# A decoder layer on one core: gate tiles as paired block products ahead of the attention, keys a head sooner, batched small operations

## The chip, the cores and the metric

The kernel runs on one core of a Trainium2 chip. The metric is the device time of one execution in microseconds; the median of three runs is compared. The engines are TensorE (PE, matmuls into PSUM), VectorE (DVE), ScalarE (ACT), GpSimd (POOL) and SyncE (SP, which issues most of the DMAs).

## The reference

One layer of a hybrid decoder over 1024 tokens with 1024 channels, in float32, with three branches that read one input projection, are gated and merged:

```python
h = rms_norm(x, norm_mix_pre[l])
proj = h @ w_in[l]
q_d, k_d, v_d, u_p, q_m, gate_logits = jnp.split(proj, split_pts, axis=-1)
...
a = diff_attention(q_d, k_d, v_d, lam)               # 8 heads, two softmax maps each, ALiBi, causal
a = rms_norm(a, subln_g[l]) * (1.0 - lam_init)
y_attn = a.reshape(B, S, DIFF_V_WIDTH).astype(x.dtype) @ w_attn_branch[l]
...
gates = jax.nn.sigmoid(gate_logits.astype(jnp.float32)).reshape(B, S, N_BRANCHES, D).astype(x.dtype)
mix = gates[:, :, 0] * y_attn + gates[:, :, 1] * y_pool + gates[:, :, 2] * y_mem
x = x + rms_norm(mix @ w_out[l], norm_mix_post[l])
```

`diff_attention` forms, per head and block of queries, two softmax maps p0 and p1 over the keys and weighs the values with p0 - lam * p1. A second half, the channel mixer (up projection, depthwise convolution of width 3, gelu gate, down projection), follows; the change doesn't touch it.

## The kernel before

**Number format.** Every large matmul is done in three passes: each operand is split into a high part (ScalarE copy to the fp32r format, line 89) and a low part (VectorE subtraction, line 90), and `mm3` (lines 102 to 105) adds high x high, high x low and low x high into PSUM. A split costs one instruction on each of the two engines.

**Stages, in order.** (1) Norm of `x` and `mem`, keys and values of the memory branch; (2) memory attention and the pooling projection; (3) the pooled and the memory branch; (4) the gates of those two branches (lines 861 to 881); (5) values of the attention (lines 957 to 997), and under them the key weights of heads 2 to 7, split and stored to DRAM (`key_weights`, line 922); (6) keys of heads 0 and 1, queries of all heads, gate tiles 0 and 1 of the attention branch (lines 1019 to 1033); (7) the attention, head by head (lines 1273 to 1346); (8) the rest of the gates, the norm of the heads and the merge (lines 1366 to 1420); (9) output projection and channel mixer.

**Block products.** Stages 4 to 6 use `seven` (line 198): a pair of 128-channel tiles times all tokens as a 2 x 2 block product with seven products instead of eight, with sums of the weights and of the tokens. Each product takes a page of 512 weights per partition, splits it, and issues 4 blocks of `mm3`. `channels` (line 999) loads the two weight tiles of a pair (`rawq`; one slot in `wst`'s tag `raw`, which has two, one in `grp`) and calls `seven`. A tile done directly (`gate`, line 1116, and `head_keys`, line 1090) takes for each half of the tokens 8 blocks of `mm3`.

**Attention.** Each head has four query blocks of 256 queries, each of two tiles of 128. `scores` (line 1140) does for one tile and both maps the matmuls into `pss`, a VectorE operation that adds the bias and takes the extreme (line 1165), and the exponential on ScalarE with its sum (line 1170). `combine` (line 1176) joins the maps of one tile with two operations on one column (lines 1181, 1182) and one over all keys (1184). `turn_weights` transposes and splits the weights (`pta`, `aT`), `weigh_values` multiplies them with `v` (`poa`), `head_norm` sums squares over channels (`pn`). `weave` spreads "fillers" between these stages: the keys of the next head (four steps of 12 matmuls), the loads of its values, and gate steps of 6 matmuls. `GATES` (line 1290) puts gate tiles 2 and 3 into head 0 and tile 4 into head 7.

**Behind the attention.** Gate tiles 5 to 7 run directly (line 1370). Each head's output `a` and its norm factor `rb`, both from DRAM, are multiplied (line 1384) and split into `ath` and `atl`. The factors of heads 4 to 7 go through `load_norms` (`hn`), about 15 small VectorE operations in `head_norms`, and a store to `r_d`, before `rb` can be read. `merge_heads` (line 1356) multiplies with `w_attn_branch`, one 128-channel tile `dt` at a time, first half of the heads (g = 0) and then the second; only tiles 0 and 1 have their first half issued ahead of the second four heads. `merge` (line 1403) gates the result, adds the other branches and splits.

**What sets the order.** The kernel is written in one order; a planner then places each instruction on its engine's queue as early as its inputs and buffers allow, with program order as the priority, so PE's gate matmuls slip into places where the attention's are not ready. `issue_after` puts an instruction behind a named one on the same engine: gate matmuls stay behind the scores that were written before them. DMAs issued by SP wait in SP's queue, one behind the other.

**Memory.** Pools are stacked; the attention's pools `qkp` (32 KB a partition: four key tiles, two query tiles), `att` and `vp` (two buffers of values of 8 KB) are closed behind it, and `atp` (`ath`, `atl`, 64 KB), then `sub` (`a` and `rb`, four buffers of 4 KB each) take their place from the same upper end down; a tile waits for the tiles on whose bytes it lies.

Of the kernel before, what the change touches and what calls it, by code (L numbers as in the profile page):

```python
# [41 lines left out]
def kernel(  # L42
# [275 lines left out]
    wk_d = dram.tile([NH, P, 2, KT, P], F32, name="wk_d")  # L318
    v_d = dram.tile([NH, P, 2, KT, P], F32, name="v_d")
# [541 lines left out]
    with tc.tile_pool(name="gp", reuse_waits="tile", bufs=2, side="right") as gp_:  # L861
# [60 lines left out]
        def key_weights(h):  # L922

            raw = wst.tile([P, KT, P], F32, tag="raw", name="rawk", bufs=2)
            with tc.issue_after(loads["v"].ins):
                nc.sync.dma_start(out=raw, in_=chunk(w_in, C_K + h * P))
            for e in range(2):
                page = wst.tile([P, 2, H4, P], F32R, tag=("wh", "wl")[pages[0] % 2], name="kpage")
                pages[0] += 1
                ks = slice(e * H4, (e + 1) * H4)  # L930
                split(page[:, 0], page[:, 1], raw[:, ks])
                nc.sync.dma_start(out=wk_d[h, :, :, ks], in_=page.bitcast(F32))
# [92 lines left out]

        ss = gp_.tile([P, 4, H4, P], F32, tag="g", name="ss", bufs=3)
# [4 lines left out]
        ready = {2: wsplit(chunk(w_in, C_G + 2 * P), [P, KT, P])}  # L1031
        with tc.issue_after(ready[2][2].ins):
            late[0]()
# [10 lines left out]
    bias = ap_.tile([P, 1152], F32, name="bias", bufs=1)  # L1044
# [5 lines left out]
    def head_bias(h):  # L1050
        biases[h] = ap_.tile([P, 1152], F32, tag="hbias", name="hbias", bufs=2)
        nc.scalar.activation(out=biases[h], in_=bias, func=AF.Copy, scale=2.0 ** -(h + 1))
# [26 lines left out]
    def key_tiles(h):  # L1079
        return [qkp.tile([P, S], F32R, tag="ks%d%d" % (c, h % 2), name="ks%d" % c) for c in range(2)]  # L1080
# [9 lines left out]
    def head_keys(h):  # L1090
# [25 lines left out]
    def gate(dt):  # L1116


        with tc.issue_after(last["load"].ins):
            wh, wl, _ = ready.pop(dt) if dt in ready else wsplit(chunk(w_in, C_G + dt * P), [P, KT, P])  # L1120
        for i in range(2):
# [18 lines left out]
    def scores(h, b, u):  # L1140
# [9 lines left out]
        sm = small.tile([P, 1], F32, tag="sm", name="sm")  # L1150
# [5 lines left out]
        for c in range(2):  # L1156
            pss = bank2(name="pss2")
            for i in range(parts):
                keys = ks[c][:, i * m:(i + 1) * m]
                for j in range(2):  # L1160
                    last["scores"] = nc.tensor.matmul(pss[:, i * H:i * H + m], q[:, j, c, ts], keys,  # L1161
                                                      start=(j == 0), stop=(j == 1))
            z = ap_.tile([P, S], F32, tag="z%d" % c, name="z", bufs=3 - c)
# [7 lines left out]
                                 bias=mx[:, c:c + 1], accum_out=sm if c else sums[:, h, t:t + 1])  # L1171
        exps[h, b, u] = z2, mx, sm
# [3 lines left out]
    def combine(h, b, u):  # L1176

        z2, mx, sm = exps.pop((h, b, u))
        t = 2 * b + u
        n = (t + 1) * P  # L1180
        nc.vector.reciprocal(out=mx[:, 1:2], in_=sm)
        nc.vector.scalar_tensor_tensor(
            out=mx[:, 0:1], in0=mx[:, 1:2], scalar=sums[:, h, t:t + 1], in1=nlam, op0=ALU.mult, op1=ALU.mult)
        last["combine"] = nc.vector.scalar_tensor_tensor(
            out=z2[0][:, 0:n], in0=z2[1][:, 0:n], scalar=mx[:, 0:1], in1=z2[0][:, 0:n],
            op0=ALU.mult, op1=ALU.add)
        zts[h, b, u] = z2[0]
# [89 lines left out]
    first = gate(2)  # L1277
# [8 lines left out]
    with tc.issue_after(last["load"].ins):  # L1286
        ready[3] = wsplit(chunk(w_in, C_G + 3 * P), [P, KT, P])
        for dt in range(2):
            nc.sync.dma_start(out=gate_d[dt], in_=g01[dt])
    GATES = ((2, 3), (), (), (), (), (), (), (4,))  # L1290
    blocks = [(h, b) for h in range(NH) for b in range(4)]
    for h in range(NH):
        stages = []
        for b in range(4):
# [10 lines left out]
            if n >= 1:  # L1305
                def weights(n=n):
                    combine(*blocks[n - 1], 1)
# [3 lines left out]
            stages.append(lambda h=h, b=b: combine(h, b, 0))  # L1311
# [15 lines left out]
        fillers = []  # L1327
        if h + 1 < NH:
            if h:
                fillers += steps(head_keys(h + 1), 4)  # L1330
            for n, step in enumerate(steps(values(h + 1), 2)):
                fillers.insert(2 * n + 1, step)
        n = 0
        for dt in GATES[h]:
            for step in steps(first if dt == 2 else gate(dt), 6 if dt == 2 else 8):
                fillers.insert(min(n, len(fillers)), step)
                n += 2
        weave(stages, fillers)
    combine(*blocks[-1], 1)
# [5 lines left out]
    load_norms(1)  # L1345
# [8 lines left out]
    pys = {}  # L1354

    def merge_heads(dt, g):
# [441 lines left out]
```

## Time and profile before

| what | value |
|---|---|
| median of three runs (lowest, highest) | 1727.77 us (1726.58, 1728.74) |
| span of the profiled execution | 1727.6 us |
| PE busy | 1712.8 us (99%) |
| VectorE busy | 1241.3 us (72%) |
| ScalarE busy | 886.6 us (51%) |
| attention, first scores to last values | 605.3 to 881.8 us |
| first merge matmul | 910.8 us |

The profiled execution's own time is the span, first to last instruction; the runs' times are measured without the profiler's page and lie around it by less than 1.2 us. In the rows of the timeline the columns are start, duration, engine, line, operation, output<-inputs, shapes and count, with idle time and its releaser in brackets. In rows that begin with a:b, a stretch of the span, the columns are its length, the busy time and number of instructions of PE, PE's weight loads, VectorE, ScalarE and GpSimd, then the granted clock, the share of the DMA engines' time and GB/s. Rows that begin with a line number are groups: durations are the least, the median and the most in ns, then the first and the last start. A matmul's recorded duration overlaps with the next one's.

### The profile page before, as it was taken

To read this page: it belongs to the slowest core of one execution; us is meant where nothing else is said; L and a number is where in the kernel's file an instruction comes from. 1 tells how busy PE (TensorE), PEld (TensorE's weight loads), DVE (VectorE), ACT (ScalarE), POOL (GpSimd) and SP (SyncE) were. 2 spreads that over 40 slices of the span, in tenths; PEclk is the share of its full clock that TensorE was granted. 3 is DMA by queue.
4 is the path that set the end of the run, shared out by engine and by line. 5 is a ranking of instruction groups with operands and counts; after the bars stand their busy time and mean duration, and the time that the engine had idled before them with its cause. 6 is when DMAs were issued, how large, how long until landed. Compare 5 with 4: busy or idle time off the path is not lost.

```text
span 1727.6 us, 22400 instructions
## 1 busy us (share of the span) xinstructions
PE 1712.8 (99%) x8106; PEld 1421.4 (82%) x8106; DVE 1241.3 (72%) x2047; ACT 886.6 (51%) x1577; POOL 45.0 (3%) x103
## 2 busy tenths in 40 slices
PE   9999999999999999999999999999999999999998
PEld 7888888887888888888888888888888888888886
DVE  6765875666665578888866555848888888878466
ACT  5434544434544467777754344645555555543453
POOL 0000000000000011111110000000000000000000
PEclk9999999999999999999999999999999999999999
DMA  8873544444874686665556571572333423583344
GB/s 273 317 281 114 163 150 133 166 147 143 266 237 159 201 231 170 176 182 152 145 187 239 176 230 50 171 225 92 124 112 107 122 85 98 190 299 106 107 149 142
DMA packets 232803, 294.41 MB, mean 170 GB/s; under 512 B 15865, under 2 KB 161526, under 8 KB 230006
## 3 DMA queue, kind: packets, MB, share of 16 engines
q1 hardware_dynamic: 229158, 285.61, 51.8%
q0 software_dynamic: 3520, 7.38, 1.2%
q8 instruction: 64, 1.05, 0.3%
q14 instruction: 45, 0.37, 0.1%
q10 hardware_dynamic: 16, 0.00, 0.0%
HBM read 201.10 MB, written 85.56 MB: 166 GB/s over the span
## 4 chain that ended last, share of the span: by engine, by line
PE 91%; DVE 5%; DMA 2%; ACT 1%; issue 1%; SPq 0%; DVEq 0%; ACTq 0%
PE pa L103 8%; PE pa L104 8%; PE pa L105 8%; PE pb L103 5%; PE pb L104 5%; PE pb L105 5%; PE pss L1161 3%; PE poa L1217 2%; PE pd L103 2%; PE pd L105 2%; PE pd L104 2%; PE pe L105 2%; PE pe L104 2%; PE pe L103 2%; PE pout L103 2%; PE pout L105 2%
## 5 line engine op out<-in xcount | busy, mean ns | idle before, releaser
L89 ACT ACTIVATE wpage<-s 128x512 fp32r<-128x512 f32 x136 | 85.3, 627 | 108.2 <-DVE s L188 35.3
L90 DVE TENSOR_TENSOR wpage<-s,wpage 128x512 fp32r<-128x512 f32 x136 | 92.8, 688 | 43.2 <-ACT wpage L89 43.2
L1565 DVE SCALAR_TENSOR_TENSOR cvt<-gv,cols,cvt 128x1023 f32<-128x1023 f32 x88 | 112.5, 1278 | 15.6 <-ACT cvt L1561 14.9
L1165 DVE CUSTOM_DVE_ANT_0 z<-pss,hbias 128x256 f32<-128x256 f32 (+7 forms) x128 | 94.5, 752 | 26.0 <-PE pss L1161 24.8
L1170 ACT ACTIVATE z<-z,mx 128x256 f32<-128x256 f32 (+7 forms) x128 | 98.8, 773 | 20.8 <-DVE mx L1165 20.7
L103 PE MATMUL pa<-T,wpage 128*128 128x512 f32 x264 | 102.8, 389 | 0.0
L105 PE MATMUL pa<-T,wpage 128*128 128x512 f32 x264 | 102.7, 389 | 0.0
L104 PE MATMUL pa<-T,wpage 128*128 128x512 f32 x264 | 102.7, 389 | 0.0
L1161 PE MATMUL pss<-ks,q 128*128 128x512 f32 (+5 forms) x384 | 86.6, 349 | 1.4 <-DVE mx L1165 1.4
L89 ACT ACTIVATE page<-blk 128x1024 fp32r<-128x1024 f32 (+1 forms) x42 | 41.4, 989 | 85.7 <-PE pe L104 50.6
L90 DVE TENSOR_TENSOR page<-blk,page 128x1024 fp32r<-128x1024 f32 (+1 forms) x42 | 47.5, 1130 | 38.1 <-ACT page L89 38.1
L1161 PEld LDWEIGHTS pss<-ks,q 128*128 128x128 f32 x384 | 62.9, 189 | 11.1 <-DVE mx L1165 6.2
L103 PE MATMUL pd<-page 128*128 128x512 f32 x176 | 68.7, 390 | 0.0
L104 PE MATMUL pd<-page 128*128 128x512 f32 x176 | 68.5, 389 | 0.0
L105 PE MATMUL pd<-page 128*128 128x512 f32 x176 | 68.3, 389 | 0.0
L103 PE MATMUL pa<-hT,wpage 128*128 128x512 f32 x168 | 65.5, 390 | 0.1
L105 PE MATMUL pa<-hT,wpage 128*128 128x512 f32 x168 | 65.4, 389 | 0.0
L104 PE MATMUL pa<-hT,wpage 128*128 128x512 f32 x168 | 65.4, 389 | 0.0
L1217 PEld LDWEIGHTS poa<-aT,v 128*128 128x128 f32 x480 | 60.7, 190 | 3.0 <-ACT srow L1237 1.4
L1217 PE MATMUL poa<-aT,v 128*128 128x256 f32 (+1 forms) x480 | 62.5, 280 | 0.0
L103 PEld LDWEIGHTS pa<-T,wpage 128*128 128x128 f32 x264 | 49.6, 188 | 10.7 <-DVE gv L250 0.3
L104 PEld LDWEIGHTS pa<-T,wpage 128*128 128x128 f32 x264 | 49.6, 188 | 10.2
(429 smaller groups left out, 4965.7 us busy)
## 6 DMA issues: line engine op xcount, KB each, us to landing
q<-q_d SPq DMA_DIRECT2D x64, 256.0 KB, 5.1
wd<-in_w_down_dram SPq DMA_DIRECT2D x22, 512.0 KB, 5.0
tw_d<-wd SPq DMA_DIRECT2D x11, 1024.0 KB
rawv<-in_w_up_dram SPq DMA_DIRECT2D x22, 512.0 KB, 5.8
rawu<-in_w_up_dram SPq DMA_DIRECT2D x22, 512.0 KB, 4.1
ff_d<-cvt SPq DMA_DIRECT2D x22, 512.0 KB, 5.4
blk<-ff_d SPq DMA_DIRECT2D x20, 512.0 KB, 7.9
br<-tw_d SPq DMA_DIRECT2D x20, 512.0 KB, 5.0
```

Source lines behind the costliest of these rows:

```text
L89: copy = nc.scalar.activation(out=hi, in_=src, func=AF.Copy)
L90: nc.vector.tensor_tensor(out=lo, in0=src, in1=hi.bitcast(F32), op=ALU.subtract)
L103: nc.tensor.matmul(o, ah, bh, start=first, stop=False, skip_group_check=onto)
L104: nc.tensor.matmul(o, ah, bl, start=False, stop=False, skip_group_check=onto)
L105: return nc.tensor.matmul(o, al, bh, start=False, stop=last, skip_group_check=onto)
L1161: last["scores"] = nc.tensor.matmul(pss[:, i * H:i * H + m], q[:, j, c, ts], keys, start=(j == 0), stop=(j == 1))
L1165: nc.vector.tensor_tensor_reduce(out=halves(z[:, 0:n]), in0=pss.rearrange("p (a m) -> p a m", a=2)[:, 0:parts, 0:m], in1=halves(biases[h][ ...
L1170: nc.scalar.activation(out=z[:, 0:n], in_=z[:, 0:n], func=AF.Exp, scale=-1.0, bias=mx[:, c:c + 1], accum_out=sm if c else sums[:, h, t:t + 1])
L1217: nc.tensor.matmul(po[:, qs], (vh, vl)[i][:, k, :], w[j][:, ws], start=(n == 0), stop=(n == len(terms) - 1))
L1565: nc.vector.scalar_tensor_tensor(out=cv[:, sh:], in0=u[:, 0:S - sh], scalar=w, in1=cv[:, sh:], op0=ALU.mult, op1=ALU.add)
```

## The change

- Gate tiles 2 and 3, and 4 and 5, are computed by two more calls of `channels`, ahead of the pair 0 and 1, and stored to DRAM from there. Tiles 6 and 7 stay direct. Their weights are split ahead, in the values' stage, by `gate_weights`, the same way as the key weights, and are loaded ready made; tile 6's first half uses a split of its own and begins ahead of the attention.
- `head_keys` gives way in steps of 6 matmuls. All steps stand in one queue (rest of the first half of tile 6, keys of heads 2 to 7, tile 6's second half, tile 7), from which the heads take 9, 7, 7, 7, 7, 7, 7 and 5 steps. The queue has 62 steps; the last 6 run behind the attention. Head 1 and later heads thus work on keys one head further ahead, for which the key tiles rotate over three sets, one of them in `wst`'s `raw` buffers.
- `combine` handles both tiles of a block at once, in the next block: one reciprocal and one product on two columns in place of two of each. The second map's `z` gets a third buffer. A head's bias is made from the one before it, and the separate `bias` tile goes.
- Behind the attention the loads of heads 0 to 3 come first, then `load_norms(1)`, the six gate steps, and the norm of these heads. `merge_heads` handles two tiles at once in units of half the heads (48 matmuls), so that four tiles (eight PSUM banks) have their first half issued ahead of the second four heads; `merge` loads its gates behind the heads' loads. `gs` is a column of a 4384-byte tile.

```diff
+        def split_ahead(c0, dst):
             raw = wst.tile([P, KT, P], F32, tag="raw", name="rawk", bufs=2)
...
+        def gate_weights(n):
+            split_ahead(C_G + (6 + n) * P, wg_d[n])
...
         value_product("T4", vblock(*A22), va, False)
+        gate_weights(0)
+        gate_weights(1)
...
+        for dt in (2, 4):
+            g = channels(C_G + dt * P)
+            nc.sync.dma_start(out=gate_d[dt:dt + 2].rearrange("e p s -> p e s"), in_=g)
...
-        ready = {2: wsplit(chunk(w_in, C_G + 2 * P), [P, KT, P])}
+        ready = {6: wsplit(chunk(w_in, C_G + 6 * P), [P, KT, P])}
...
-                if k == H4:
+                if k in (2, 4, 6):
                     yield
...
+            z = ap_.tile([P, S], F32, tag="z%d" % c, name="z", bufs=3)
...
-    GATES = ((2, 3), (), (), (), (), (), (), (4,))
+    queue = steps(first, 2)
+    for h in range(2, NH):
+        queue += steps(head_keys(h), 8)
+    queue += steps(gate(6, (1,)), 4) + steps(gate(7, (0, 1)), 8)
+    SHARES = (9, 7, 7, 7, 7, 7, 7, 5)
...
+    def combine(h, b):
+
+        both, sm = exps.pop((h, b))
+        nc.vector.reciprocal(out=sm, in_=sm)
+        nc.vector.scalar_tensor_tensor(
+            out=sm, in0=sm, scalar=nlam, in1=sums[:, h, 2 * b:2 * b + 2], op0=ALU.mult, op1=ALU.mult)
+        for u, (z0, z1) in enumerate(both):
...
+        for h in range(HG):
+            load_head(h)
+        load_norms(1)
+        for step in queue:
+            step()
+        merge_weights(0, 0)
+        for h in range(HG):
+            normed_head(h)
+        merge_weights(1, 0)
+        with tc.issue_after(ends["square"].ins):
+            head_norms(1)
+        merge_heads(0, 0)
+        merge_weights(0, 1)
+        merge_heads(1, 0)
+        merge_weights(1, 1)
+        for h in range(HG, NH):
+            load_head(h)
+            normed_head(h)
```

More of the change, by code (lines that the diff above doesn't have):

```diff
@@ L1276 @@
     load_keys(0)
-    first = gate(2)
+    first = gate(6, (0,))
     head_bias(0)
@@ L1306, in weights @@
                 def weights(n=n):
-                    combine(*blocks[n - 1], 1)
+                    combine(*blocks[n - 1])
                     turn_weights(*blocks[n - 1])
@@ L1344 @@
     head_norm(*blocks[-1])
-    load_norms(1)
     cstack.close()
```

129 lines of the change are left out of this document (66 added, 63 removed).

## The prediction

> **What bounds the kernel now.** I read the page's engine shares first, then its chain of waits, then the tensor engine's own waits.
>
> ```profile
> span 1727.6 us, 22400 instructions
> PE 1712.8 (99%) x8106; PEld 1421.4 (82%) x8106; DVE 1241.3 (72%) x2047; ACT 886.6 (51%) x1577; POOL 45.0 (3%) x103
> ...
> PE 91%; DVE 5%; DMA 2%; ACT 1%; issue 1%; SPq 0%; DVEq 0%; ACTq 0%
> ```
>
> The tensor engine is busy in 99% of the span and carries 91% of the chain. A change pays only if it takes matmuls away or takes a wait away from PE, and it costs wherever PE finds nothing to do. The price of a matmul isn't its duration, because matmuls overlap. The next fence shows PE's timeline at the end of the stage ahead of the attention, then two stretches with the busy time of each engine.
>
> ```profile
> 602.60 0.39 PE L103 MATMUL pg<-hTh,wh 128*128 128x512 f32 x1
> 602.83 0.39 PE L104 MATMUL pg<-hTl,wh 128*128 128x512 f32 x1
> ...
> 409.60:487.70 78.10, 77.22 (x335) 62.06 (x334) 56.21 (x78) 40.02 (x68) 0.00 (x0) 1.00 0.82 254
> 487.70:605.30 117.60, 117.60 (x520) 97.39 (x519) 65.81 (x93) 51.33 (x80) 2.81 (x3) 1.00 0.58 188
> ```
>
> A matmul lasts 0.39 us, but the next starts 0.23 us later; 520 of them in 117.60 us make 0.226 us each, and PE has no gap there. So 0.226 us is the price.
>
> **1. Block products: -5.4 us.** A gate tile done directly is 2 halves x 8 blocks x 3 passes = 48 matmuls, so tiles 2 to 5 are 192. A pair by `seven` is 7 products x 4 blocks x 3 passes = 84, so two pairs are 168. 24 matmuls go: 24 x 0.226 = 5.4 us. The pairs' extra work on VectorE and ScalarE (sums, splits, evictions), four weight loads and two 1 MB stores stand beside PE as those of the four query pairs do now: that stretch has VectorE busy 65.81 of 117.60 us and PE never waiting. If that cover failed, each pair would wait for one weight load, 3.7 to 4.8 us by the landing row quoted in part 2.
>
> **2. Weights of tiles 6 and 7 split ahead: +1.5 us (0 to 4).** These are two loads, four splits and four stores, put behind the last value product. The splits fit: VectorE has 22 us free in 409.60:487.70 and they need 4 x 0.69 = 2.8. But the load of the key pair's first weights now has to come after them, as there are two `raw` slots.
>
> ```profile
> 463.15 0.56 SPq L1004 DMA_DIRECT2D rawq<-in_w_in_dram  x1
> ...
> 472.70 0.69 DVE L90 TENSOR_TENSOR kpage<-rawk,kpage 128x512 fp32r<-128x512 f32 x1 [0.69 <-ACT kpage L89]
> ...
> 477.28 0.39 PE L103 MATMUL vd<-vpage,hT 128*128 128x512 f32 x1
> ...
> 488.36 0.39 PE L103 MATMUL pa<-hTh,wpage 128*128 128x512 f32 x1
> ...
> DMA to landing us min/median/max: 3.7/3.7/4.8
> ```
>
> Today that load is issued at 463.15 (its landing is the last row). After the change tile 6's weights take the slot at that time. Its two pages take the slots of the value product's first two pages, which PE holds for 2.8 us each from 477.28: so they are split at about 481.4 and 484.1. The key pair's load follows at 484.2, lands at 488 to 489, and its split (0.6 on ScalarE) is done by 488.6 to 489.6, where PE wants it at 488.36: 0.2 to 1.2 us late. The value stores stand in the same SP queue and may hold the load up to 3 us more. Queued behind PE's wait is the whole key pair. I take 1.5.
>
> **3. The attention itself: -1.5 us (-6 to +6).** Heads 1 to 6 have 48 key matmuls each as fillers now; after it, seven steps of six, 42. Head 0 goes from 84 to 54. The next fence has the stretch of heads 1 to 6, head 7 up to its last scores, the rest of head 7, and then the two small operations of `combine`; the last two rows are the chain in one head.
>
> ```profile
> 641.70:838.00 196.30, 194.30 (x1204) 168.93 (x1203) 168.55 (x446) 148.15 (x365) 25.63 (x48) 1.00 0.64 175
> ...
> 838.00:866.60 28.60, 27.43 (x166) 23.54 (x165) 23.99 (x62) 21.51 (x53) 4.30 (x8) 1.00 0.41 114
> 866.60:881.80 15.20, 15.20 (x98) 12.64 (x97) 10.30 (x19) 9.15 (x20) 2.12 (x4) 1.00 0.23 64
> ...
> L1181 DVE RECIPROCAL mx<-sm x64: 142/158/165, 607.4 to 870.3; 128x1 f32<-128x1 f32 x64
> ...
> L1182 DVE SCALAR_TENSOR_TENSOR mx<-mx,sums,nlam x64: 119/219/221, 607.6 to 871.8; 128x1 f32<-128x1 f32 x64
> ...
> 659.04 0.73 DVE z L1165
> ...
> 675.61 0.98 PE pta L1200 x7
> ```
>
> A head takes 32.7 us (196.30 / 6) and keeps VectorE busy 28.1. Six matmuls fewer make it 31.3; halving eight pairs of small operations takes 4 x (0.158 + 0.219) = 1.5 us off VectorE, 26.6. The ratio stays at 0.85 to 0.86, so I expect much the same small waits, less what the third `z1` buffer, keys a head sooner and the gate weight splits gone from head 7 save. The chain runs on VectorE from 659.04 to 675.61, so late in a head VectorE already leads: fewer fillers can also lay 1 us of it bare per head, +6. PE's gaps in the first two rows are 2.0 and 1.2 us; as its busy time counts overlapped ends, the waits can be twice that, and -6 is all of them gone.
>
> **4. The seam behind the attention: +10 us (+4 to +17).** This decides. The next fences show PE's `pg` (gate) matmuls in the last stretch of head 7 and behind it, PE's last values and first merge, then SP, VectorE and one row of ScalarE there.
>
> ```profile
> 866.60:881.80 15.20, 8.68 (x31) 5.29 (x32) 0.00 (x0) 0.60 (x1) 1.00 0.23 64
> 881.80:910.80 29.00, 28.90 (x126) 23.37 (x126) 0.00 (x0) 2.93 (x5) 1.00 0.80 285
> ...
> 878.93 3.00 PE L1217 MATMUL poa<-aT,v 128*128 128x256 f32 x24
> ...
> L103 PE MATMUL pya<-ath,wh x128: 389/389/389, 910.8 to 997.2; 128*128 128x512 f32 x128
> ...
> L1412 DVE TENSOR_TENSOR gm<-pya,gm x16: 682/684/692, 924.6 to 999.2; 128x512 f32<-128x512 f32 x16
> ```
>
> ```profile
> 886.91 0.36 SPq L1255 DMA_DIRECT2D hn<-ss_d  x1
> 887.38 0.45 SPq L1381 DMA_DIRECT2D a<-ao_d  x1
> ...
> 895.51 0.37 SPq L1267 DMA_DIRECT2D r_d<-hn  x1
> ...
> 903.49 0.33 SPq L1383 DMA_DIRECT2D rb<-r_d  x1
> ...
> 893.64 1.28 DVE L1384 SCALAR_TENSOR_TENSOR a<-a,gs,rb 128x1024 f32<-128x1024 f32 x1 [0.40 <-DMA rb<-r_d]
> ...
> 894.96 1.06 ACT L89 ACTIVATE ath<-a 128x1024 fp32r<-128x1024 f32 x1 [4.39 <-DVE a L1384]
> ...
> 897.20 1.28 DVE L1384 SCALAR_TENSOR_TENSOR a<-a,gs,rb 128x1024 f32<-128x1024 f32 x1
> ...
> 904.43 2.44 DVE L90 TENSOR_TENSOR atl<-a,ath 128x1024 fp32r<-128x1024 f32 x2
> ...
> 922.13 1.23 DVE L90 TENSOR_TENSOR atl<-a,ath 128x1024 fp32r<-128x1024 f32 x1 [1.13 <-ACT ath L89]
> ```
>
> Call te the end of the last values, 881.8. Between the last scores and te the chain exp, combine, transposes, values takes 15.2 us, in which 31 gate matmuls (31 x 0.226 = 7.0) fill what PE's own attention work leaves. Then 126 more gate records, 28.9 us, cover the way to the normed heads, and the merge starts at 910.8.
>
> After the change six steps of tile 7 are left, 36 matmuls, 8.1 us. They are ready when the last scores are issued and fill the hole before te, as the 31 do now; 1.1 us of them is left at te, and then the merge wants head 0.
>
> I expect that head 0 can't be there. Counted down from the upper end of these pools, keys, queries and the attention's buffers take 91.25 KB, then come 8 KB of the last head's `v`; the normed heads (64 KB), `rb` (16) and `a` (16) put the lowest buffer of `a` at 92 to 96 KB, on that `v`. If head 0 takes it, its load starts at te; SP isn't held by `hn` any more, which is 5.5 us sooner than the 887.38 of today. From that issue to the first normed multiply are 6.3 us (893.64), and from there to head 3's split 13.2 us (904.43 + 2.44 - 893.64; the second head follows 3.56 us later). So head 3 is ready at te + 19.5, and PE's last 12 matmuls of the first half-merge need 2.7 more: te + 22.2 for 48 matmuls that are 10.9 us long. That is 11.3 us of waiting. Less the 1.1 that is left of tile 7 it is 10.2; I take 10, by the measured pace. The lower end: three of the four `a` and all `rb` are loaded before te, and head 0 takes one of the free buffers, so that only what lies on `v` waits: a load of 4 us, 1.28 + 1.06 + 1.23 of work, te + 7.6, and PE gets there after 1.1 + 3 x 2.7 = 9.2 if that head comes last in order; with it second, 1.1 + 2.7 = 3.8, it waits 4. The upper end is today's order of loads, `hn` first: 5.5 more, with the rest 17.
>
> Late next would be heads 4 to 7: today their last split ends at 923.4, te + 41.5. The doubled first halves (four tiles, 96 matmuls, 21.8 us) bring PE to them at te + 22.2 + 10.9 = 33.1, and to head 7's part 8.2 later, 41.3: just in time, at no cost. Four evictions at once are 4 x 3 x 0.69 = 8.3 us of VectorE behind 10.9 us of matmuls; uncovered they would cost 2 to 3.
>
> The trace can't show what a gap of 8 us does to PE's clock: the granted clock is 1.00 in every stretch quoted. [...]
>
> **Sum.** 1727.6 - 5.4 + 1.5 - 1.5 + 10 = 1732.2. The profiled span of 1727.6 stands 0.2 below the median of the runs, 1727.77, so nothing is added: 1732.
>
> **Rivals.**
> The seam is covered (faster). SP issues before te the loads whose buffers are free by then, the four `rb` on `z` and the `a` on bias buffers, and head 0 has one of these; the seam costs its lower end, 4, the values' seam 0, and the attention loses 5 of its waits: 1727.6 - 5.4 + 4 - 5 = 1721. For it: those buffers are free with the last softmax, some 8 us ahead of te, and the DMA engines are used to 0.23 there. Against it: SP issued `a` and `rb` strictly in turn. It wins where the first normed multiply starts before te + 2.
> The gain is eaten exactly: seam 6, the rest 0: 1728.
> Late heads (slower still). `hn` is loaded after eight 512 KB loads instead of ahead of them. Behind such loads the small `r_d` store of 895.51 released its reader only at 903.49, 8 us. So long a delay moves heads 4 to 7 by 7: 1739. It decides once `hn` lands later than te + 8.
> The heads become VectorE's: +1 us each, 1732 + 1.5 + 6 = 1740, if busy VectorE in a head passes 0.9 of its time.
>
> **How the numbers follow.** Forecast 0.42, seam covered 0.31, gain eaten 0.12, late heads 0.10, VectorE's heads 0.05. A measurement tells 0.2%, 3.5 us. Faster is the covered seam, 0.31. No change is the eaten gain and the low part of the forecast, 0.12 + 0.07 = 0.19 (a seam under 9 is no change). Slower is the rest, 0.50. The range leaves a tenth on each side: 1719 to 1740; the forecast's own is 1729 to 1737.
>
> **What would show it.** 24 matmuls fewer, and the four pairs ahead of the attention without a gap in PE. PE idle for 6 to 9 us right after the last `poa`, ended by `ath` or `atl`, then gaps of about 1 us at every fourth of the first half-merge. A head of 31 us. A gap of 1 to 2 us before the key pair's first product. I'm wrong if PE has less than 3 us of gaps between the last scores and the second half-merge; if it has 17 or more, the loads stand in the wrong order.

## The result and the profile after

The changed kernel is slower: 1781.14 us, median of four runs (1778.97 to 1783.26), against 1727.97 for the kernel before. The ratio is 1.0306, 95% interval 1.0291 to 1.0321. The forecast was 1732 with a range up to 1740; the direction was right, the size was not. The profiled execution spans 1777.6 us, 50.0 more than the one before. First its page:

```profile
span 1777.6 us, 22326 instructions
PE 1724.5 (97%) x8082; PEld 1419.9 (80%) x8082; DVE 1246.4 (70%) x2010; ACT 892.5 (50%) x1590; POOL 40.9 (2%) x95
...
PE 82%; DVE 7%; DMA 6%; ACT 3%; issue 1%; SPq 1%; DVEq 0%; ACTq 0%
```

24 matmuls are gone, yet PE is busy 11.7 us longer, and it has fallen from 91% to 82% of the chain; DMA has come from 2% to 6%. Next the stretches from the values' end on, in the kernel before and then in the changed one: pairs and queries, attention, the part up to the last merge matmul, and the output projection. Columns are as in the prediction.

```profile
475.00:605.30 130.30, 130.30 (x575) 107.66 (x574) 77.67 (x112) 57.75 (x92) 2.81 (x3) 1.00 0.63 199
605.30:881.90 276.60, 272.55 (x1656) 235.65 (x1655) 228.83 (x591) 201.94 (x491) 36.51 (x68) 1.00 0.61 168
881.90:997.60 115.70, 115.70 (x512) 95.56 (x511) 67.47 (x91) 46.03 (x62) 4.32 (x8) 1.00 0.67 227
997.60:1090.00 92.40, 92.40 (x433) 76.98 (x432) 51.34 (x98) 38.29 (x74) 0.00 (x0) 1.00 0.37 122
```

```profile
475.00:605.30 130.30, 114.58 (x483) 92.81 (x483) 73.54 (x108) 53.00 (x85) 0.00 (x0) 0.92 0.54 178
605.30:939.60 334.30, 323.51 (x1838) 271.09 (x1837) 240.09 (x560) 218.12 (x517) 37.85 (x68) 0.99 0.60 167
939.60:1042.60 103.00, 90.98 (x391) 73.73 (x390) 62.47 (x86) 39.27 (x53) 1.63 (x3) 0.93 0.66 222
1042.60:1139.00 96.40, 93.39 (x433) 76.67 (x432) 53.43 (x101) 39.12 (x76) 0.00 (x0) 1.00 0.41 128
```

In the first and the third stretch PE now stands still for 15.7 and 12.0 us, where before it had no gap, and the granted clock falls to 0.92 and 0.93 there. (The second stretch of the changed kernel holds the two new pairs too, up to 662.)

Busy time hides short waits, since it counts overlapped ends (a matmul with 512 columns lasts 0.39 us by its record, and the next starts 0.23 us later). So from here on I count **excess**: the distance from one matmul's start to the next, less the usual one of its kind (0.227 us for most with 512 columns, 0.118 for 256, 0.109 for a transpose), summed over a stretch. It takes in waits and a slow clock.

| stretch | before, us | after, us | difference |
|---|---|---|---|
| start to 475, in the value products | 10.5 | 9.0 | -1.5 |
| 475 to 605: key pair and query pairs | 0.0 | 20.8 | +20.8 |
| 605 to the last values: (gate pairs,) attention | 14.0 | 30.3 | +16.3 |
| last values to the last merge matmul | 0.1 | 14.9 | +14.8 |
| output projection | 0.1 | 4.2 | +4.1 |
| rest | -0.4 | -0.2 | +0.2 |

Together +54.7; less 5.4 for 24 matmuls that is 49.3 of the 50.0 us.

### The profile page after: what moved, and what is told of

It is laid out like the page before. It is cut to its first block, busy times and chain, and to the rows that moved or that the text cites. A ratio compares the mean times of both kernels' runs of the same rounds, so it can differ in the third digit from the quotient of the medians.

```text
span 1777.6 us, 22326 instructions
## 1 busy us (share of the span) xinstructions
PE 1724.5 (97%) x8082; PEld 1419.9 (80%) x8082; DVE 1246.4 (70%) x2010; ACT 892.5 (50%) x1590; POOL 40.9 (2%) x95
## 4 chain that ended last, share of the span: by engine, by line
PE 82%; DVE 7%; DMA 6%; ACT 3%; issue 1%; SPq 1%; DVEq 0%; ACTq 0%
PE pa L103 8%; PE pa L104 8%; PE pa L105 8%; PE pb L105 5%; PE pb L104 5%; PE pb L103 5%; PE pss L1183 3%; PE poa L1239 2%; PE pd L103 2%; PE pd L105 2%; PE pd L104 2%; PE pe L105 2%; PE pe L104 2%; PE pe L103 2%; PE pta L1222 2%
## 5 line engine op out<-in xcount | busy, mean ns | idle before, releaser
L89 ACT ACTIVATE wpage<-s 128x512 fp32r<-128x512 f32 x144 | 90.3, 627 | 115.5 <-DVE s L188 44.6
L90 DVE TENSOR_TENSOR wpage<-s,wpage 128x512 fp32r<-128x512 f32 x144 | 98.2, 688 | 48.3 <-ACT wpage L89 48.1
L1183 PE MATMUL pss<-ks,q 128*128 128x512 f32 (+5 forms) x384 | 92.9, 353 | 2.3 <-DVE mx L1187 2.1
L103 PE MATMUL pa<-hT,wpage 128*128 128x512 f32 x192 | 75.0, 391 | 0.2 <-ACT wpage L89 0.2
L104 PE MATMUL pa<-hT,wpage 128*128 128x512 f32 x192 | 74.9, 390 | 0.0
L105 PE MATMUL pa<-hT,wpage 128*128 128x512 f32 x192 | 74.7, 389 | 0.0
L103 PE MATMUL pya<-ath,wh 128*128 128x512 f32 x128 | 50.0, 396 | 11.9 <-ACT ath L89 11.9
L103 PEld LDWEIGHTS pa<-T,wpage 128*128 128x128 f32 x264 | 49.5, 188 | 10.7 <-DVE gv L250 0.4
```

Source lines behind the costliest of these rows:

```text
L89: copy = nc.scalar.activation(out=hi, in_=src, func=AF.Copy)
L90: nc.vector.tensor_tensor(out=lo, in0=src, in1=hi.bitcast(F32), op=ALU.subtract)
L103: nc.tensor.matmul(o, ah, bh, start=first, stop=False, skip_group_check=onto)
L104: nc.tensor.matmul(o, ah, bl, start=False, stop=False, skip_group_check=onto)
L105: return nc.tensor.matmul(o, al, bh, start=False, stop=last, skip_group_check=onto)
```

## The experiments

Each run is compared with the kernel before on the same chip, whose median was 1727.9 to 1728.7 in all of them.

### The key pair's load: a1, a2 and c1

The changed kernel at the values' end: SP's queue, the split that frees the first gate tile's buffer (DVE) and one of the second gate tile's splits (ACT), then PE's first products of the key pair:

```profile
475.93 0.89 SPq L927 DMA_DIRECT2D rawk<-in_w_in_dram  x1
...
483.68 3.96 SPq L933 DMA_DIRECT2D wg_d<-kpage  x2
487.69 2.46 SPq L960 DMA_DIRECT2D v_d<-vout  x3
490.25 0.82 SPq L933 DMA_DIRECT2D wg_d<-kpage  x1
491.11 4.12 SPq L960 DMA_DIRECT2D v_d<-vhl  x4
495.28 0.86 SPq L1013 DMA_DIRECT2D rawq<-in_w_in_dram  x1
...
497.01 3.30 SPq L960 DMA_DIRECT2D v_d<-vhl  x4
500.36 1.79 SPq L1013 DMA_DIRECT2D rawq<-in_w_in_dram  x2
...
482.97 0.68 DVE L90 TENSOR_TENSOR kpage<-rawk,kpage 128x512 fp32r<-128x512 f32 x1
...
485.73 0.63 ACT L89 ACTIVATE kpage<-rawk 128x512 fp32r<-128x512 f32 x1 [3.39 <-DMA wg_d<-kpage]
...
501.08 0.79 PE L103 MATMUL pa<-hTh,wpage 128*128 128x512 f32 x1 [13.96 <-ACT wpage L89]
507.91 0.50 PE L103 MATMUL pb<-hT,wpage 128*128 128x512 f32 x1 [1.34 <-ACT wpage L89]
```

In the kernel before the key pair's first load (`rawq`) went out at 463.15. In the changed one it goes out at 495.28, behind the second gate tile's load, its stores and the value stores, and PE waits 13.96 us. **a1_in_place** takes the work away, **a2_among_queries** moves it:

```diff
-        gate_weights(0)
-        gate_weights(1)
...
-                    nc.sync.dma_start(out=w.bitcast(F32), in_=wg_d[dt - 6, :, e])
+                wh, wl, _ = wsplit(chunk(w_in, C_G + dt * P), [P, KT, P])        # a1
...
             split_heads(channels(h * P), q_d[h:h + 2], -0.125)
+            if h in (2, 4):                                                       # a2
+                gate_weights(h // 2 - 1)
```

> The changed kernel without gate_weights: the weights of gate tiles 6 and 7 are split when they are needed, as in the kernel before. Changed kernel: 1781 us, with one PE wait of 14.1 us at 486.7 ahead of the key pair and a PE clock of 0.61 to 0.83 until 520. Theory 'one load stands too late in SP's queue' (the key pair's first weights, issued at 495.28 instead of 463.15, behind the gate weights' loads and stores): the wait and the slow clock behind it go, 14.1 + 6.5 us, so about 1760, perhaps 1 to 3 us more for the splits that come back into head 7. Rival 'the four gate pairs ahead of the attention load the DMA queues or VectorE': the pairs stay, so the wait stays, about 1781.

> The changed kernel with the same gate_weights work moved behind the second and the third query pair. Theory 'the order in SP's queue': the same 2 MB loads, splits and 2 MB stores cost nothing there, since VectorE and the DMA engines have room in the query products; about 1760 to 1763, as without the work. Rival 'the amount of the work, wherever it is put' (4 MB more on the DMA queues, pages taken from the products): a good part of the 20 us comes back as waits among the query pairs, 1770 or more.

Measured: 1760.18 us (1.0187, 1.0172 to 1.0202) and 1759.72 us (1.0185, 1.0170 to 1.0200). The stretch of PE's wait, in the changed kernel, then in a1, then in a2:

```profile
486.00:502.00 16.00, 2.04 (x7) 1.27 (x7) 4.76 (x7) 3.90 (x7) 0.00 (x0) 0.61 0.95 292
502.00:510.00 8.00, 6.25 (x17) 4.17 (x17) 3.50 (x6) 2.74 (x5) 0.00 (x0) 0.71 0.55 159
```

```profile
486.00:502.00 16.00, 16.00 (x72) 13.27 (x71) 7.62 (x12) 6.75 (x12) 0.00 (x0) 1.00 0.82 234
```

```profile
486.00:502.00 16.00, 16.00 (x72) 13.26 (x71) 8.27 (x13) 6.69 (x12) 0.00 (x0) 1.00 0.81 230
```

21 us go in both. The same loads, splits and stores cost nothing among the query pairs, so it was their place, not their amount. That the place counts through SP's queue is read from the rows above: the load's buffer is free at 483.65, and the load goes out 11.6 us later.

**c1_busy** asks how much of the 20.8 us is PE's slow clock:

```diff
         gate_weights(1)
+        spare = pbank(name="spare")
+        for k in range(60):
+            nc.tensor.matmul(spare, hTh[0][:, k % KT, 0:P], hTh[1][:, k % KT, :], start=True, stop=True)
```

> The changed kernel with 60 matmuls (13.6 us) on a spare PSUM tile between the last value product and the key pair; their result is not used. They stand where PE waits 14.1 us, and behind that wait PE's granted clock is 0.61 (486 to 502), 0.71 (502 to 510) and 0.83 (510 to 520), which costs 6.5 us against the usual pitch, 2.7 of them shown as further waits. Theory 'the clock falls because PE is idle': the key pair starts at the same time and runs at full clock, so 4 to 6 us less than the changed kernel, about 1775 to 1777. Rival 'the slow matmuls behind the wait are late operands': no change, 1779 to 1783.

Measured: 1778.9 us (1778.33 to 1783.17; 1.0301, 1.0285 to 1.0317). The granted clock did stay up, at 1.00 from 486 to 502; the time didn't follow. c1's stretches and its first products:

```profile
486.00:502.00 16.00, 14.31 (x63) 11.26 (x61) 4.07 (x7) 2.95 (x6) 0.00 (x0) 1.00 0.94 279
502.00:510.00 8.00, 5.54 (x18) 3.86 (x18) 4.71 (x9) 2.90 (x5) 0.00 (x0) 0.83 0.48 138
```

```profile
501.34 0.50 PE L103 MATMUL pa<-hTh,wpage 128*128 128x512 f32 x1 [1.69 <-ACT wpage L89]
506.71 0.50 PE L103 MATMUL pb<-hT,wpage 128*128 128x512 f32 x1 [2.10 <-ACT wpage L89]
```

The granted clock is 0.83 for 0.71, but the second product starts only 1.2 us sooner, since it needs the second weights, loaded at 500.36 in the changed kernel (500.33 here). From 475 to 605 the 13.6 us of extra matmuls and the excess that is left, 6.5, make 20.1 for 20.8. So the slow clock stood mostly beside a wait for late operands; my theory missed.

### Head 0's fillers: a3

In the changed kernel the weights of head 2's keys are asked for behind the query loads, and the first key matmul of the attention comes at 694.5, 25 us after the last gate matmul that could fill. SP's queue and one of PE's waits there, then the group of the key matmuls with its first and last start:

```profile
668.22 2.48 SPq L1089 DMA_DIRECT2D q<-q_d  x4
671.06 0.33 SPq L1111 DMA_DIRECT2D wh<-wk_d  x1
...
684.80 0.55 PE L1222 MATMUL pta<-ident,z 128*128 128x128 f32 x3 [1.09 <-DVE aT L90]
```

```profile
L103 PE MATMUL pqk<-hTh,wh x96: 387/395/485, 694.5 to 887.0; 128*128 128x512 f32 x96
```

**a3_whole6** is a1 with tile 6, whose weights are split ahead, wholly in head 0:

```diff
-    first = gate(6, (0,))
+    first = gate(6, (0, 1))
...
-    queue = steps(first, 2)
+    queue = steps(first, 6)
...
-    queue += steps(gate(6, (1,)), 4) + steps(gate(7, (0, 1)), 8)
-    SHARES = (9, 7, 7, 7, 7, 7, 7, 5)
+    queue += steps(gate(7, (0, 1)), 8)
+    SHARES = (12, 7, 7, 7, 7, 7, 7, 2)
```

> As a1_in_place, and gate tile 6 runs wholly (both halves) as filler of head 0, ahead of the keys of head 2; shares 12,7,7,7,7,7,7,2. Changed kernel: PE has 11 us of waits from 640 to 707, where from 669.4 to 694.5 no filler runs, because the weights of head 2's keys are issued at 671. Theory 'head 0 has no filler that is ready': those waits fall by 6 to 9 us against a1_in_place, and head 7 with three steps fewer gives back up to 5; about 1753 to 1759. Rival 'VectorE leads in the first head, whatever PE has to fill': the same as a1_in_place, about 1760.

Measured: 1751.79 us (1.0135, 1.0118 to 1.0152), 8.4 less than a1. From the last value product to the end of head 0's share the excess falls from 11.7 to 5.7 us, as expected. But heads 6 and 7 give back 1.9, and 6.1 us more came from the seam behind the attention, which I hadn't expected: there the order of the loads had changed (next part). The key weights' place in the queue is not what a3 changed: they are asked for at 651.45 (650.03 in a1), and the first key matmul comes at 672.6 (674.0). It is ready gate matmuls that fill head 0.

### The seam behind the attention: a4, e3 and e4

The end of the attention in the changed kernel, whose last values end at 939.6: SP's queue, the first normed multiply, PE's first merge, and the stretches behind it. Then the same steps in a3, where they end at 915.2.

```profile
942.92 0.38 SPq L336 DMA_DIRECT2D raw<-in_w_attn_branch_dram  x1
943.47 0.38 SPq L1399 DMA_DIRECT2D a<-ao_d  x1
...
951.04 1.28 DVE L1406 SCALAR_TENSOR_TENSOR a<-a,gs,rb 128x1024 f32<-128x1024 f32 x1 [8.08 <-DMA rb<-r_d]
...
953.47 1.22 PE L103 MATMUL pya<-ath,wh 128*128 128x512 f32 x2 [11.87 <-ACT ath L89]
```

```profile
942.00:955.00 13.00, 1.49 (x3) 0.78 (x4) 3.80 (x5) 1.54 (x3) 1.06 (x2) 0.56 0.83 299
955.00:960.00 5.00, 5.00 (x18) 4.02 (x19) 3.29 (x3) 1.61 (x2) 0.00 (x0) 0.78 0.98 361
960.00:1010.00 50.00, 50.00 (x222) 41.02 (x221) 32.08 (x48) 18.80 (x24) 0.00 (x0) 1.00 0.56 186
```

```profile
915.22 0.34 SPq L1395 DMA_DIRECT2D a<-ao_d  x1
...
920.38 1.28 DVE L1402 SCALAR_TENSOR_TENSOR a<-a,gs,rb 128x1024 f32<-128x1024 f32 x1
...
922.81 1.22 PE L103 MATMUL pya<-ath,wh 128*128 128x512 f32 x2 [4.65 <-ACT ath L89]
```

In the changed kernel the second merge weights' load (`raw`, 942.92) stands ahead of the heads' in SP's queue and waits for its buffer, which the first merge weights' split frees at 942.90; the heads' loads start 3.9 us behind the last values, and the merge 13.9. In a3 that load has gone ahead long before; the heads' loads start with the last values, and the merge 7.6 later. **a4_early_heads** moves both on the changed kernel: heads 0 and 1 get buffers that are free at the last transposes, and the second merge weights are loaded behind the heads.

```diff
+            ta, tr = (("y", "rb"), ("rb", "rb"), ("w", "rb"), ("x", "x"))[h % 4]
...
+        first = {h: sub.tile([P, S], F32, tag=t, name="a", bufs=bufs[t]) for h, t in ((3, "x"), (0, "y"), (2, "w"))}
...
-        merge_weights(1, 0)
+        with tc.issue_after(marks["head"].ins):
+            merge_weights(1, 0)
```

> The changed kernel with other buffers for the normed heads behind the attention: heads 0 and 1 get those that are free at the last transposes, ahead of the last values, and the second merge weights are loaded behind the heads' loads. Changed kernel: loads from 943.5, 3.9 us behind the last values, PE waits 12.1 us and runs at half clock after it. Theory 'the loads start late': they start at about 938, PE's wait falls to 3 to 6 us and the clock loss of 2 us goes with it; 1770 to 1773. Rival 'DMA engines bound it' (4 MB for four heads at 430 GB/s are 10 us): heads 2 and 3 come at the same time as now, and the waits are only shifted to the later heads; 1778 to 1781.

Measured: 1776.59 us (1.0280, 1.0265 to 1.0295), 4.5 less. The loads start 1.4 us ahead of the last values, and the excess up to the first merge falls from 12.7 to 6.4; but 4.8 us of new waits stand further on in the merge, and 0.7 more at its start. So of 6.3 us won at the first merge 5.5 come back, as the rival said, and the seam gains 0.8. The two profiled executions are 3.3 us apart, and 2.2 of these stand at the key pair (18.7 us for 20.9), which this edit doesn't touch.

What did the old kernel's gate matmuls at this place do? **e3_onepair** is the kernel before with one pair ahead, **e4_loads_first** is e3 with the heads' loads ahead of `load_norms(1)`:

```diff
             split_heads(channels(h * P), q_d[h:h + 2], -0.125)
+        g = channels(C_G + 2 * P)
+        nc.sync.dma_start(out=gate_d[2:4].rearrange("e p s -> p e s"), in_=g)
...
-    GATES = ((2, 3), (), (), (), (), (), (), (4,))
+    GATES = ((4, 5), (), (), (), (), (), (), (6,))
...
-        for dt in range(5, KT):
+        for h in range(HG):                                                       # e4
+            load_head(h)
+        load_norms(1)
+        for dt in range(7, KT):
```

> The kernel before with gate tiles 2 and 3 as one pair of block products ahead of the attention, tiles 4 and 5 as fillers of head 0, 6 in head 7 and 7 behind it; nothing else. 12 matmuls fewer, -2.7 us, and 96 fewer of cover behind head 7's scores: of the 28.9 us of gate matmuls behind the last values some 7 stay. Theory 'the 28.9 us of cover are needed as long as heads are loaded behind the norms': PE waits 15 to 21 us there, 1740 to 1747. Rival 'the pairs are free and the cover was ample': 1724 to 1727.

> As e3_onepair, and the loads of heads 0 to 3 stand ahead of the norms' load, as in the changed kernel. Loads from about the last values on, head 0 ready 7.6 us later as in a3_whole6, some 7 us of cover: PE waits 1 to 3 us there and 2 to 4 us more for heads 1 to 3 (3.56 us each against 2.7 of matmuls per pair of tiles, 1.4 per tile here, so up to 8), heads 4 to 7 late by up to 10. 1733 to 1742. Rival 'with the loads first the seam is covered': 1725 to 1728, which would beat the kernel before.

Measured: 1738.55 us (1.0060, 1.0046 to 1.0073) and 1744.91 us (1.0099, 1.0085 to 1.0113). PE's first merge in e3 (last values 898.7), then in e4 (900.5) with the second half-merge:

```profile
913.04 1.22 PE L103 MATMUL pya<-ath,wh 128*128 128x512 f32 x2 [7.03 <-ACT ath L89]
```

```profile
912.28 0.73 PE L103 MATMUL pya<-ath,wh 128*128 128x512 f32 x2 [4.46 <-ACT ath L89]
...
936.69 1.65 PE L103 MATMUL pya<-ath,wh 128*128 128x512 f32 x3 [10.19 <-ACT ath L89]
```

In e3 the attention has the excess of the kernel before to within 0.6 us in each head, and the pair itself has no wait: a pair ahead is free. The cover that it takes is not: 13.4 us of excess up to the last merge matmul, for 2.7 us of matmuls. That is a little under my 15 to 21. In e4 the first merge comes sooner, and the wait moves to heads 4 to 7, 10.2 us, because `hn` now stands behind the bulk loads: the factors' store `r_d` goes out at 926.05, for 912.47 in e3. In the changed kernel it is as late, 13.8 us behind the first merge, but the doubled first halves keep PE at work until 977.5, and head 4's normed multiply starts at 973.5.

### Batching: b1, e2, d2 and e1

**b1_batched** is the kernel before with the batched `combine`, the third `z1` buffer and the chained bias; **e2_third** has the buffer and the bias without the batching. **d2_unbatched** is a3 without the batching, and **e1_best** is d2 with the heads' loads ahead of the second merge weights and d3's buffers (below). The edit of b1 (d2 takes the batching back; e2 has the `z` line and the bias):

```diff
+            exps[h, b] = [], small.tile([P, 2], F32, tag="sm", name="sm")
-            z = ap_.tile([P, S], F32, tag="z%d" % c, name="z", bufs=3 - c)
+            z = ap_.tile([P, S], F32, tag="z%d" % c, name="z", bufs=3)
...
-            stages.append(lambda h=h, b=b: combine(h, b, 0))
```

> The kernel before with only the batched small operations: combine for both tiles of a block, the second map's z with a third buffer, a head's bias from the one before it. No change of gates, keys or of the part behind the attention. Theory 'VectorE work off the heads shortens PE's waits': the waits of 605 to 884, 14.8 us, fall by 1 to 4 us, 1724 to 1727. Rival 'combine of a block's first tile comes later now, so the chain of each block starts later': waits grow by 0.3 to 0.5 us a head, 1730 to 1732, as in the changed kernel, whose middle heads wait 1.8 to 2.2 us each in place of 1.4.

> The kernel before with only the third buffer of the second map's z and the bias made from the one before; no batching. Theory 'b1_batched lost by the batching': no change, 1726 to 1729. Rival 'it lost by the third buffer, or by the bias chain': 1731 to 1733.

> As a3_whole6 (1751.8 us), with combine for each tile by itself again, as in the kernel before (the third buffer and the bias stay). Theory from b1_batched (batching made the kernel before 4.7 us slower): a block's first tile is joined earlier again and the transposes come sooner, 3 to 6 us less, 1746 to 1749. Rival 'in b1_batched it was the third buffer or the bias, not the batching': 1750 to 1754.

> a3_whole6 (1751.8 us) with combine for each tile by itself, the pool for the merge's gate loads, and the second merge weights loaded behind the normed heads' loads. In d2_unbatched the attention was 5 us shorter, but the second merge weights' load stood ahead of the heads' loads (915.2, 4.8 us behind the last values) and PE waited 12.2 us instead of 4.8. Theory 'batching costs the attention 5 us, and it was hidden by the order of loads': 5 us from the attention, 5 from the output projection, seam as in a3_whole6; 1740 to 1743. Rival 'the seam's wait is the time from the last scores, whatever the order': the seam stays at 12 us, 1747 to 1750.

Measured: b1 1732.6 us (1.0028, 1.0016 to 1.0039), e2 1727.42 (0.9998, 0.9989 to 1.0007), d2 1752.1 (1.0141, 1.0125 to 1.0157), e1 1745.96 (1.0101, 1.0083 to 1.0120). b1 from 605.30 to its last values, to set against 605.30:881.90 of the kernel before (b1's first scores stand at 603.1 already):

```profile
605.30:885.10 279.80, 273.61 (x1648) 234.21 (x1647) 219.04 (x519) 201.71 (x486) 36.52 (x68) 1.00 0.60 165
```

VectorE works 9.8 us less, and from first scores to last values the attention takes 5.4 us longer. Its excess rises from 13.8 to 18.6, while e2 has 12.6: the batching is what costs, not the buffer. In a3 taking it out brings the attention's excess from 27.7 to 22.8. A block's first tile is joined later: the median time from the end of its second map's exponential to the joining is 5.3 us in b1, 3.2 in e2 and 2.2 in the kernel before. Most of the price stands in one place, between head 5's last values and head 6's: 6.0 us in b1 for 3.1 before, and 4.4 in d2 for 7.8 in a3. d2's time shows nothing of that, because there the second merge weights' load again stands ahead of the heads' (915.2, 4.8 us behind the last values) and the first merge waits 12.0 us. In e1, with that order held, the wait is 5.2; but new waits of 3.9 us stand further on in the merge, and e1's runs lie far apart (1741.37 to 1749.54), above the 1740 to 1743 of my expectation for the most part.

### The rest: c3, d1, d3, c4 and d4

```diff
+            if (h, b) == (6, 2):                                                  # c3
+                    ready[7] = wsplit(chunk(w_in, C_G + 7 * P), [P, KT, P])
...
-                mm3(pq, wh[:, k, :], wl[:, k, :], hTh[i][:, k, :], hTl[i][:, k, :], k == 0, k == KT - 1)
+                with tc.issue_after(last["scores"].ins):                          # d1
+                    mm3(pq, wh[:, k, :], wl[:, k, :], hTh[i][:, k, :], hTl[i][:, k, :], k == 0, k == KT - 1)
...
-            gm2 = gq.tile([P, 2, H], F32, tag="t", name="gm2")
+            gm2 = gmp.tile([P, 2, H], F32, tag="t", name="gm2")                   # d3, pool of three
```

> As a3_whole6 (1751.8 us), and the weights of gate tile 7 are asked for ahead of head 7's second query loads. a3_whole6 has 7.8 us of PE waits in head 6 and 3.8 in head 7, between the last key matmul and the first gate matmul. Theory 'the fillers stand still because their weights are asked for behind the query loads in SP's queue': 4 to 6 us of these waits go, about 1746 to 1748. Rival 'two query blocks without enough matmuls for VectorE's chain, whatever the loads': no change, 1750 to 1753.

> As a3_whole6 (1751.8 us), and each key matmul stays behind the scores that were written before it, as the gate matmuls do. In a3_whole6 the keys of head 7 are used up at 867.8, 16 us ahead of the end of head 6 (PE waits 7.8 us in it). Theory 'the fillers run ahead and are used up': they last longer, and the waits of head 6 fall by 3 to 5 us, of the heads ahead of it by 0 to 0.5 each; 1746 to 1749. Rival 'VectorE's chain is longer than PE's work in such a head, however its matmuls are spread': the waits move, but stay, 1750 to 1754.

> As a3_whole6 (1751.8 us), with a pool of three buffers of its own for the merge's gate loads, and nothing else. c4_seam, which had this and the early buffers, had no wait ahead of the output projection (0.1 us for 6.2), but 2 us more in the merge. Theory 'two buffers for four evictions at a time': 6 us less with nothing given back, 1745 to 1747. Rival 'PE's later arrival is paid elsewhere, in loads of the output weights': 1750 to 1752.

> As a3_whole6 (1751.8 us), with the early buffers of a4_early_heads and a pool of three buffers of its own for the merge's gate loads in place of the two of gq. Theory: the seam's wait falls by 2 to 4 us, and the waits ahead of the output projection (6 us in a3_whole6), if they come from the two buffers, by 3 to 6 us: 1743 to 1747. Rival 'the merge's last four evictions on ScalarE and VectorE are too many, whatever the buffers': the 6 us stay, 1748 to 1750.

> a3_whole6 with the three edits of d1_hold, d2_unbatched and d3_gmpool at once. If each removes what its theory says and they stand in different places, their sum: 12 to 16 us less than a3_whole6, 1736 to 1740; still above the kernel before, since the waits behind the last values (5 us), in the first half of the merge (3 us) and a few us in heads 0 to 6 stay. If the attention's waits only move, 1744 to 1747.

Measured: c3 1751.66 us (1.0135, 1.0121 to 1.0149), d1 1759.24 (1.0176, 1.0158 to 1.0195), d3 1746.85 (1.0112, 1.0096 to 1.0128), c4 1750.61 (1.0131, 1.0117 to 1.0144), d4 1755.96 (1.0164, 1.0147 to 1.0180).

c3, d1, c4 and d4 miss what I expected. With its weights early the last gate tile helps head 6 no more (8.0 us of excess for 7.8), and key matmuls held behind the scores make heads 1 to 5 worse (3.2 to 4.7 us for 1.6 to 2.6). Here running fillers ahead is better than holding them.

d3 gives 4.9 us. PE's waits ahead of the output projection in the changed kernel (its weight loads):

```profile
1049.30 0.19 PEld L103 LDWEIGHTS pout<-woh,mixh 128*128 128x128 f32 x1 [1.34 <-ACT woh L89]
1051.02 0.19 PEld L104 LDWEIGHTS pout<-wol,mixh 128*128 128x128 f32 x1 [1.54 <-DVE wol L90]
```

Their excess is 6.2 us in a3, 2.2 in d3 and 0.1 in c4: four evictions at a time through two buffers hold back the splits of the output weights (the third buffer and the pool of its own came together; no run parts them). c4 adds a4's early buffers to d3 and ends no better: up to the first merge it has the excess of a3 (4.9 for 5.1), and it has 2.0 more further on and 1.9 more in head 6. d3 has 1.5 more there too, and neither edit touches the attention: the three kernels with the same attention (a3, d3, c4) have 7.8, 9.3 and 9.7 in head 6. d4 has the edits of d1, d2 and d3 together, and it has d1's loss in the heads and d2's wait at the seam.

No version beats the kernel before; the best of the changed ones, e1 and d3, are 1.0 to 1.1% above it. In e1 8.7 us more than before are left in the attention and 12.3 from the last values to the last merge matmul, for the 5.4 of the matmuls saved.

## Why the prediction was right or wrong

**Block products, -5.4: right.** 24 matmuls fewer, and neither the two pairs here nor e3's one pair make PE wait.

**Weights of tiles 6 and 7 ahead, +1.5 (0 to 4): wrong, and the largest miss, 20.8 measured, 21 by a1 and a2.** The part that held: the load had to come after the gate weights' splits, and tile 6's second split ended at 483.65, near the 484.1 to 484.2 that I counted. The part that failed was "The key pair's load follows at 484.2", with up to 3 us more for the value stores. I took the moment at which the buffer becomes free for the moment of the issue. Ahead of the load SP's queue still had the second gate tile's two stores, the last of which went out at 490.25, and seven value stores; it went out 11 us later. SP waited 2.7 us of these for the second gate tile's split, which itself waited for a store of the first to land (485.73); the nine stores behind that wait took 8.1 us to go out. And I left out the second weights of the pair, loaded at 500.36 behind four more value stores, which hold up the second product until 507.9. In the 2.7 us that SP waited (484.4 to 487.1) the load stood behind a store that waited, while its own buffer was free.

**Attention, -1.5 (-6 to +6): wrong, +16.3 in excess.** The step that failed is "I expect much the same small waits". By place it is 8.7 us in head 0, 2.4 in heads 1 to 5 together, 3.2 in head 6 and 2.0 in head 7. Two causes are shown by runs. 6.0 us are head 0's missing fillers (a1 to a3), of which heads 6 and 7 take 1.9 back: I had counted head 0's matmuls (54 for 84) and not when they can run. Why the keys of head 2 can't fill there isn't shown: the second part of their weights, asked for at 672.15 behind the query loads, landed 10.5 us later, and the first key matmul came only at 694.5. 4.9 are the batching (a3 against d2; b1 has 6.0 more than e2, and its time is 5.2 longer). I priced that as 1.5 us of VectorE per head saved; VectorE's time was saved (9.8 us in b1), but a block's first tile is now joined with the second, so the chain's steps come later, and PE waits. With both out, in d2, the attention still has 9.0 us more than before, half of them in head 0; that fewer fillers are the cause fits the prediction's upper end, but no run shows it by itself.

**Seam, +10 (+4 to +17): right in kind, 14.8 in size, and inside the range partly by luck, since the upper end stood for `hn` first in the queue.** Head 0's buffer was the one on the last values, as I took it, and PE stood still right behind the last `poa`, ended by `ath`. In a3 the loads start with the last values and the merge comes 7.6 us later, near the 6.3 and a split that I counted. The changed kernel adds 3.9 us for the merge weights' load ahead of the heads' in the queue and some 2 of slower landing beside it (7.6 us from first load to first multiply for 5.2 in a3). d2 and e1, which differ in that order and in d3's buffers, show the same: 12.0 us of wait at the first merge for 5.2, of which 3.9 come back further on. I had expected gaps at every head, which was wrong: once PE had begun, at a granted clock of 0.50 up to 957.0, it followed the heads without a further wait of note. What the gap does to PE's clock the trace of before couldn't show, and the sum has no term for it: 2.2 us of excess stand in the 12 us from the first merge on, where the rows show clocks of 0.56 and 0.78.

**Evictions, "at no cost", "2 to 3 if uncovered": 4.1.** At the last pair nothing covers them, which I saw as a condition and didn't check. A pool of its own with three buffers takes 4.0 of a3's 6.2 away (d3).

**The rivals.** "Seam covered" didn't come, and the late heads of `hn` behind bulk loads came in e4 (10.2 us) but not here, where the doubled halves hide them by the times above. None of the rivals, nor the range, held a load that starves PE ahead of the attention: all my cases but the heads on VectorE, which didn't come (VectorE is busy 121.59 of the 144 us from 740 to 884), stood at the seam, and three of the places that lost were elsewhere.

## What to carry to other kernels

The moment at which a buffer becomes free is a lower bound of a load's issue, no more (here 483.65, and the issue 495.28): write down everything that stands ahead of it in its queue, with what each of these waits for and how long it takes to go out, above all where work has been put in front of it. A batch of operations is worth its engine's time only where that engine is the bound; where a chain runs through it, what counts is when the first result leaves (in b1 VectorE worked 9.8 us less and the attention took 5.4 us longer). And matmuls that stand in another stage's waits are cover: the kernel before needed its gate matmuls just where it had them, and taking 96 away to save 12 cost five times the gain (13.4 for 2.7 us).

## What the runs showed of the hardware

Keeping PE busy through a wait of 14 us (c1) held its granted clock at 1.00 from 486 to 502, for 0.61 in the changed kernel, and brought it to 0.83 instead of 0.71 in the stretch behind, 502 to 510, and yet gained 2.2 us at most, less than the runs' spread, since the operands were as late as before. Here the slow clock behind the wait was next to no price (20.1 us in c1 for 20.8), because PE's operands were late.

In a3 the clock also fell, to 0.89, between 870 and 900, around the end of head 6, where PE stands still for 4.1 us in all. In the changed kernel head 6 ends 20.7 us later. First a3, then the changed kernel at its head 6's end:

```profile
870.00:900.00 30.00, 25.95 (x146) 21.32 (x144) 24.99 (x59) 22.16 (x56) 3.78 (x7) 0.89 0.40 115
```

```profile
884.00:905.00 21.00, 18.38 (x111) 14.78 (x110) 14.69 (x36) 13.02 (x34) 1.58 (x3) 1.00 0.61 183
```

PE stands still about as much in both, 4.1 of 30 us and 2.6 of 21; the clock is 0.89 in one and 1.00 in the other. So the share of the time in which PE stands still (0.14 and 0.12) doesn't tell it alone, and what does is not shown. Part of a3's 7.8 us of excess in head 6 stands in the slow stretch; how much of that is the waits and how much the clock, no run takes apart.
